# A two-layer attention and retention trunk on one core: the last projection's pairs prepared earlier, its weights' sums in three supertiles, the final squares in SBUF

## The chip, the core and the metric

The kernel runs on one core of a Trainium2 chip. The core has TensorE (PE in the profile: matmuls, and PEld for the loading of their stationary operand), VectorE (DVE), ScalarE (ACT), GpSimd (POOL), and SyncE (SP), whose queue issues all of this kernel's DMAs. Every engine works through its own instructions in order; they meet at semaphores. The metric is device time in microseconds, the median of several executions; less is better.

## The reference, cut to what matters

```python
def hybrid_layer(x, norm_gain, w_in, w_out, rel_bias, cos, sin):
    hn = rms_norm(x, norm_gain)
    proj = hn @ w_in
    aq, ak, av, ag, rq, rk, rv, rg = jnp.split(proj, cuts, axis=-1)
    ya = chunked_rel_attention(aq, ak, av, rel_bias)          # 8 heads x 64
    yr = chunkwise_retention(rq, rk, rv, cos, sin)            # 4 heads x 128
    y = jnp.concatenate([ya * silu(ag), yr * silu(rg)], axis=-1)
    return x + y @ w_out

def reference(x, positions, norm_gain, w_in, w_out, rel_bias, final_gain):
    cos, sin = rotary_tables(positions, RET_HEAD_DIM)
    for layer in range(2):
        x = hybrid_layer(x, norm_gain[layer], w_in[layer], w_out[layer], rel_bias[layer], cos, sin)
    return rms_norm(x, final_gain)
```

2048 tokens, model width 1024, w_in 1024 x 4096 and w_out 1024 x 1024 for each layer.

## The kernel before

Every dense product is made of three f16 matmuls (upper half by upper half, upper by lower, lower by upper) that sum in f32 in PSUM. The tokens are cut into 16 tiles of 128 and four supertiles of 512 (`n` = 0 to 3). A layer runs over four groups of heads (`s` = 0 to 3), and in each over the supertiles: `dense_T` (12 rounds of 8 matmuls), then `dense_V` (12 rounds). `run` steps such a generator, and with each of its rounds one step of the attention of the supertile before (`attention`, 24 steps; 8 units of a token tile and a head), one step of what `later` has put off, and one step of a background generator from `push`, which prepares weights. So the instructions of PE, ACT, DVE and POOL stand in an order written out by hand, round by round. SP's order is the scheduler's, except that DMAs wrapped in `in_turn` keep their program order.

An attention unit puts its scores in PSUM (tile `S`, one buffer; line 838), DVE moves them out (849), ACT makes the exponentials (852, 854), POOL the lower halves (855), a DMA transposes them (857), PE multiplies by v (865 to 867), DVE divides and gates (877), and the result goes to `y_d` in DRAM (880; retention's at 958).

The last layer's projection, `x + y @ w_out`, is made of two-by-two blocks with seven products instead of eight (`PRODS`, line 1192). For it a *pair* is two token tiles; there are 8 pairs, and each of the seven products of a pair is 12 matmuls of 512 columns. `fast_out` runs pair after pair in `R` = 12 rounds of 7 matmuls each. Its seven left operands are blocks of y or sums of them (`A11`, `A22`, `S1`, `S2`, `S5`, `S6`, `S7`). The chain that makes a pair's operands:

- `pair_y`: two loads of y from `y_d` (1243); `pair_x`: two of x (1310).
- `sq`: ACT squares y and sums (1256); `scale`: five small operations on DVE (1260 to 1263); `mul`: ACT scales y (1268).
- `sum`: POOL makes the five sums (1286). `rows`: ACT makes the f16 upper half of a block (1296) in a tile of a ring of three (`tabc`, `tabs`, `swp`; `rowring`). `lower`: DVE, for `S1` POOL, makes the lower half (1300). `turn`: a DMA transposes both halves (1303) into one of two areas `u.T`, used by even and odd pairs; the eighth block of an area is `u.spare`.

The products are taken out of PSUM by DVE (`add_to`, 1431) and, for a second use of four of them, by ACT with an add on POOL (`by_copy`, 1438 and 1439). `final` then squares and sums the finished tile on ACT (212), with a result that nobody reads (`junk`) in a PSUM tile of tag `S`, takes the root on DVE and POOL (217, 219), scales on DVE (1018) and stores (1019).

In `fast_out` the dictionary `plan` (1392) says in which round of pair p a step of the chain of pair p + 1 stands: `sq` in rounds 0 and 1, the `turn`s in rounds 5 to 11, the loads of x in 8, and in 9 and 10 the loads of y for pair p + 2. The chain of pair 0 is made by `pair_first`, in the background of supertile 3 of the last group. With `slow` = 2 the attention of that supertile takes one step in every second round of `fast_out`: 48 rounds, pairs 0 to 3.

The right operands are blocks of w_out and their sums. `fast_weights` makes three big tiles of them (`B11`/`D21`, `T6`/`B22`, `T1`/`T7`) in the background of supertile 2: for each of four column parts two loads of 512 KB, four operations on POOL (1213, 1215, 1216), three on ACT (1220), three on DVE (1222). `pair_first` makes `D12` in supertile 3, with a difference on POOL (1326).

Of the kernel before, what the change touches and what calls it, by code (L numbers as in the profile page):

```python
# [27 lines left out]
def hybrid_trunk(ctx: ExitStack, tc: tile.TileContext, x, pos, gain, gcol, w_in, w_out, rel, fgain,  # L28
# [794 lines left out]
    def attention(l, s, n, g, st, prev):  # L823
# [36 lines left out]
        def pv(u):  # L860
            t = 4 * n + u.a
            o = psR.tile([P, 512], F32, tag="small", name=f"o{u.nm}")
            for b, (q_, a_) in enumerate(u.kts):
                v_ = q_.v[:, a_, u.hx, :]
                pe.matmul(o[:, 0:65], u.p[:, b, :], v_[:, 0:65], start=(b == 0), stop=False)  # L865
                pe.matmul(o[:, 0:64], u.p[:, b, :], v_[:, 65:129], start=False, stop=False)  # L866
                pe.matmul(o[:, 0:65], u.p[:, u.nb + b, :], v_[:, 0:65], start=False, stop=(b == u.nb - 1))  # L867

            def out_():
                rl = b2.tile([P, 1], F32, tag="rl", name=f"rl{u.nm}")  # L870
                dve.reciprocal(rl, o[:, 64:65])  # L871
                dve.tensor_tensor(rl, rl, g.ka, op=ALU.mult)
                if u.hx == 0:
                    ya[u.a] = b2.tile([P, P], F32, tag="ya", name=f"ya{u.nm}")
                y = ya[u.a]
                vs = slice(u.hx * 64, u.hx * 64 + 64)
                dve.scalar_tensor_tensor(out=y[:, vs], in0=o[:, 0:64], scalar=rl[:, 0:1], in1=st.g[u.a][:, vs],
                                         op0=ALU.mult, op1=ALU.mult)
                if u.hx == 1:
                    later(1, lambda: in_turn(sp.dma_start(y_d[t][:, s * P:(s + 1) * P], y)))  # L880

            later(1, out_)
# [3 lines left out]
        for i, (a, hx) in enumerate(units):  # L886
            flow(1)
            u = qk(a, hx)
            for r in range(3 * i, 3 * i + 3):
# [4 lines left out]
                yield  # L894


    def products(out_, pairs):
# [11 lines left out]
    def retention(l, s, n, g, st):  # L909
        for a in range(4):  # L910
# [43 lines left out]
            def fin(t=t, a=a, r2=r2, ss=ss, nm=nm):  # L954
                y = b1.tile([P, P], F32, tag="yr", name=f"yr{nm}")
                dve.scalar_tensor_tensor(out=y, in0=r2[:, 0:P], scalar=ss[:, 0:1], in1=st.g[a][:, P:256],
                                         op0=ALU.mult, op1=ALU.mult)
                later(1, lambda: in_turn(sp.dma_start(y_d[t][:, 512 + s * P:512 + (s + 1) * P], y)))

# [234 lines left out]

    def fast_weights(l, fw, go):

        big = [hT[l, 0], hT[l, 1], (b3.tile([P, KT, 512], F16, tag="wh", name=f"whF{l}"),
                                    b3.tile([P, KT, 512], F16, tag="wl", name=f"wlF{l}"))]
        h = KT // 2
        for (hi, lo), names in zip(big, (("B11", "D21"), ("T6", "B22"), ("T1", "T7"))):  # L1200
            for i, nm in enumerate(names):
                fw.w[nm] = (hi[:, i * h:(i + 1) * h, :], lo[:, i * h:(i + 1) * h, :])
        for j in range(4):
            js = slice(j * P, (j + 1) * P)
            st = []
            for c in range(2):
                st += load_sec(w_out[l, :, c * 512 + j * P:c * 512 + (j + 1) * P], f"F{l}_{j}{c}")
            st = [st_[0] for st_ in st]
            yield
            yield  # L1210
            tm = w4.tile([P, KT, P], F32, tag="w4", name=f"tmF{l}_{j}")
            for k in range(2):
                pool.tensor_tensor(tm[:, k * h:(k + 1) * h], st[0][:, k * h:(k + 1) * h], st[1][:, h:KT], op=ALU.add)
            yield
            pool.tensor_tensor(st[0][:, h:KT], st[0][:, h:KT], st[0][:, 0:h], op=ALU.subtract)
            pool.tensor_tensor(st[1][:, 0:h], st[1][:, 0:h], st[0][:, 0:h], op=ALU.add)
            srcs = (st[0], st[1], tm)
            for i in range(4):
                if i < 3:
                    act.activation(big[i][0][:, :, js], srcs[i], AF.Copy, scale=go.os[:, 0:1])  # L1220
                if i > 0:
                    dve.scalar_tensor_tensor(out=big[i - 1][1][:, :, js], in0=srcs[i - 1], scalar=go.os[:, 0:1],
                                             in1=big[i - 1][0][:, :, js], op0=ALU.mult, op1=ALU.subtract)
                if i < 3:
                    yield

# [7 lines left out]
    def pair_y(l, u, k):  # L1234
        t = u.t + k
        if k == 0:
            u.y = []
# [20 lines left out]
    def pair_scale(u, k, go):  # L1258
        m = u.m[k]
        dve.tensor_scalar(m, m, 2.0 ** -100, None, op0=ALU.max)  # L1260
        sy, iy = norm_scale(m, f"{u.nm}_{k}", None, 13)
        sc = b2.tile([P, 1], F32, tag="osc", name=f"osc{u.nm}_{k}", bufs=4)
        dve.tensor_tensor(sc, iy, go.oi, op=ALU.mult)
        u.s.append(sy)
        u.sc.append(sc)

# [44 lines left out]

    def pair_first(l, u, fw, go, areas):

# [10 lines left out]
        def diff(j):  # L1324
            a = st[j]
            pool.tensor_tensor(a[:, 0:h], a[:, 0:h], a[:, h:KT], op=ALU.subtract)

# [53 lines left out]

    def fast_out(l, fw, go, u, areas):

        NP = NT // 2
        R = 12
        events = {}
        nxt = pair(l, 1)
        for k in range(2):
            pair_y(l, nxt, k)
        pair_x(l, u)  # L1390
        mm = [(i, kt, w) for i in range(7) for kt in range(KT // 2) for w in range(3)]
        plan = {0: (("sq", 0),), 1: (("sq", 1), ("scale", 0)), 2: (("scale", 1), ("mul", 0)), 3: (("mul", 1), ("rows", "A11")),
# [29 lines left out]
        for p in range(NP):  # L1422
            if nxt is not None:
                pair_area(nxt, areas)
            after = pair(l, p + 2) if p + 2 < NP else None
            x1, x2 = u.x
# [14 lines left out]
            for r in range(R):  # L1441
                for fn in events.pop((p, r), ()):
                    fn()
                if ring["att_done"] and r % 3 == 1:
                    flow()
                assert r != 9 or p < 4 or ring["att_done"]
                for what, k in plan[r]:
                    if what == "y":
                        if after is not None:
                            pair_y(l, after, k)  # L1450
                    elif nxt is not None:
                        steps[what](nxt, k)

# [4 lines left out]
                for m in range(7 * r, 7 * r + 7):  # L1458
# [31 lines left out]
                    elif i == 5:  # L1490
                        add_to(x1, 0, ps, s1)
                        final(u.t, x1, at)
                    else:
                        add_to(x2, 1, ps, s2)
                        final(u.t + 1, x2, at)
                yield
            u, nxt = nxt, after
        for key in sorted(events):
# [249 lines left out]
    for l in range(DEPTH):  # L1748
# [4 lines left out]
        for s in range(NSW):  # L1753
            g = grp(l, s)
            for n in range(NS):
# [37 lines left out]
                if last:  # L1793
# [3 lines left out]
                    else:  # L1797
                        u0 = pair(l, 0)
                        push(pair_first(l, u0, fw, go, areas), 24)
                if not first:  # L1800
# [14 lines left out]
        if l + 1 == DEPTH:  # L1815
            ring["fg"] = cp.tile([P, D], F32, tag="gb", name="fg")
            sp.dma_start(ring["fg"], fgain.to_broadcast([P, D]))
            run(fast_out(l, fw, go, u0, areas), att, 96, 2)
            continue
# [80 lines left out]
```

## Time and profile before

| | us |
|---|---|
| median of 3 runs | 2153.07 |
| lowest and highest run | 2149.65, 2157.38 |
| the profiled execution's own time | 2152.09 |
| its span, first to last instruction | 2150.3 |

| engine | busy us | share of the span |
|---|---|---|
| PE | 1998.6 | 93% |
| DVE | 1297.6 | 60% |
| ACT | 1192.0 | 55% |
| POOL | 827.3 | 38% |

The last supertiles of the last group lie at about 1715 to 1777 us (n = 1), 1777 to 1838 us (n = 2) and 1838 to 1901 us (n = 3); `fast_out`'s first product starts at 1901.0 us and its last matmul at 2136.7 us. These bounds are read from the first and last instructions of lines 1213 (1777.4 us), 1326 (1852.7 us) and 1469 (1901.0 us). The views used below: the busy times by stretch (columns: stretch in us, its length, busy us of PE, PEld, DVE, ACT and POOL with instruction counts, granted PE clock, share of the DMA engines, GB/s); the waits (who waited for whom: total us, times, longest); the timeline (start us, duration us, engine, line, operation, and in brackets the idle time before with what ended it); the groups of instructions by line (busy us, mean ns, idle before); and the answers for one line or tile (duration ns min/median/max).

### The profile page before, as it was taken

The numbers are of one execution on the slowest core, as the hardware profiler recorded it, in microseconds if no ns is written. First come the engines' busy times: TensorE is split into PE (matmuls) and PEld (weight loads), VectorE is DVE, ScalarE is ACT, GpSimd is POOL, SyncE is SP. The second block draws the span as 40 slices with busy tenths as digits, with TensorE's granted clock in tenths as the row PEclk, the third lists the DMA queues.
The fourth block names the chain that finished last, engine by engine and source line by source line (L and its number), as shares of the span: only waits on it lengthen the run. The fifth ranks groups of instructions, "written<-read, shape, count | busy, mean of one in ns | idle before, by whom it ended". The sixth has DMA issues, their size and how long they took to land. (4 is left out here: it accounts for less than half of the span.)

```text
span 2150.3 us, 39602 instructions
## 1 busy us (share of the span) xinstructions
PE 1998.6 (93%) x13930; PEld 1046.4 (49%) x13930; DVE 1297.6 (60%) x3877; ACT 1192.0 (55%) x2622; POOL 827.3 (38%) x800
## 2 busy tenths in 40 slices
PE   6898999999999999989999999999999998876676
PEld 4444455555555555444445555555555554433332
DVE  7776656565556556766535565556556646656565
ACT  7556665465656545555445465556665645555444
POOL 1333333334433343310024433443334436554554
PEclk9999999999999999999999999999999999998888
DMA  8787765555676556998655475547485635756675
GB/s 230 166 165 161 159 136 123 115 142 127 140 162 154 129 118 124 201 254 236 185 142 121 101 156 118 115 105 155 117 184 115 150 83 134 167 136 172 154 192 146
DMA packets 675208, 322.05 MB, mean 150 GB/s; under 512 B 484640, under 2 KB 631584, under 8 KB 675008
## 3 DMA queue, kind: packets, MB, share of 16 engines
q1 hardware_dynamic: 675008, 319.51, 64.7%
q8 instruction: 109, 1.79, 0.4%
q14 instruction: 91, 0.75, 0.1%
HBM read 125.36 MB, written 41.98 MB: 78 GB/s over the span
## 5 line engine op out<-in xcount | busy, mean ns | idle before, releaser
L855 POOL TENSOR_TENSOR pq<-sc,pq 128x640 f16<-128x640 f32 (+4 forms) x256 | 321.2, 1255 | 859.5 <-ACT pq L854 469.2
L852 ACT ACTIVATE sc<-sc,mq,cT 128x640 f32<-128x640 f32 (+4 forms) x256 | 218.4, 853 | 597.9 <-DVE rl L871 273.3
L797 PE MATMUL dV<-whV,hTh 128*128 128x512 f16 x1024 | 353.3, 381 | 12.1 <-DVE gt L815 9.4
L778 PE MATMUL dT<-hTh,whT 128*128 128x512 f16 x1008 | 348.3, 381 | 6.0 <-DVE gt L815 2.8
L797 PE MATMUL dV<-whV,hTl 128*128 128x512 f16 x1024 | 353.1, 380 | 0.0
L797 PE MATMUL dV<-wlV,hTh 128*128 128x512 f16 x1024 | 352.9, 380 | 0.0
L778 PE MATMUL dT<-hTl,whT 128*128 128x512 f16 x1008 | 346.6, 379 | 0.0
L778 PE MATMUL dT<-hTh,wlT 128*128 128x512 f16 x1008 | 346.6, 379 | 0.0
L797 PEld LDWEIGHTS <-hTh 128*128 128x128 f16 x2048 | 196.7, 98 | 226.3 <-DVE gt L815 12.3
L778 PEld LDWEIGHTS <-whT 128*128 128x128 f16 x2016 | 192.5, 98 | 211.8 <-issue 3.3
L849 DVE CUSTOM_DVE_ANT_0 sc<-S,bias 128x640 f32<-128x640 f32 (+4 forms) x256 | 188.3, 735 | 84.8 <-PE S L846 83.1
L854 ACT ACTIVATE pq<-sc 128x640 f16<-128x640 f32 (+4 forms) x256 | 171.5, 670 | 8.1
L845 PE MATMUL S<-k,q 128*128 128x128 f16 (+3 forms) x592 | 143.9, 269 | 32.0 <-ACT fj L212 30.5
L797 PEld LDWEIGHTS <-hTl 128*128 128x128 f16 x1024 | 99.3, 98 | 113.5 <-issue 4.6
L778 PEld LDWEIGHTS <-wlT 128*128 128x128 f16 x1008 | 97.2, 98 | 114.2 <-issue 6.8
L865 PE MATMUL o<-v,pT 128*128 128x65 f16 x1120 | 130.5, 194 | 18.0 <-DVE ssf L217 9.9
L865 PEld LDWEIGHTS <-pT 128*128 128x128 f16 x1120 | 106.0, 97 | 55.8 <-DMA pT<-pq 12.9
L952 POOL TENSOR_TENSOR rss<-rss,mhalf 128x1 f32<-128x1 f32 x128 | 74.8, 585 | 147.1 <-DVE rss L951 139.0
L846 PE MATMUL S<-k,q 128*128 128x128 f16 (+3 forms) x592 | 131.3, 270 | 0.0
L866 PE MATMUL o<-v,pT 128*128 128x64 f16 x1120 | 130.7, 195 | 0.0
L867 PE MATMUL o<-v,pT 128*128 128x65 f16 x1120 | 129.9, 193 | 0.0
L811 DVE SCALAR_TENSOR_TENSOR v<-dV,v 128x128 f16<-128x128 f32 x128 | 36.5, 285 | 140.6 <-ACT rv L807 129.8
(489 smaller groups left out, 4016.9 us busy)
## 6 DMA issues: line engine op xcount, KB each, us to landing
q<-qq SPq DMA_DIRECT2D x128, 128.0 KB, 2.4
stT<-in_w_in_dram SPq DMA_DIRECT2D x27, 512.0 KB, 4.8
stV<-in_w_in_dram SPq DMA_DIRECT2D x26, 512.0 KB, 4.6
k<-kk SPq DMA_DIRECT2D x128, 64.0 KB, 2.0
swp<-rot SPq DMA_DIRECT2D x64, 128.0 KB, 3.0
tabc<-tab SPq DMA_DIRECT2D x32, 256.0 KB, 3.0
tabs<-tab SPq DMA_DIRECT2D x32, 256.0 KB, 3.1
swp<-raw SPq DMA_DIRECT2D x64, 128.0 KB, 2.3
```

Of the source, the lines that this page charges most:

```text
L778: pe.matmul(ps, w_[:, j, kt, :], h_[:, kt, :], start=(m == 0), stop=(m == 23))
L797: pe.matmul(ps, h_[:, kt, a * P:(a + 1) * P], w_[:, kt, :], start=(m == 0), stop=(m == 23))
L845: pe.matmul(o, st.q[:, hx, 0, cs], k_, start=True, stop=False)
L846: pe.matmul(o, st.q[:, hx, 1, cs], k_, start=False, stop=True)
L849: dve.tensor_tensor_reduce(out=v, in0=S[:, 0:w], in1=g.bias[hx][:, 640 - w:640], scale=1.0, scalar=-3.0e38, op0=ALU.add, op1=ALU.max, accu ...
L852: act.activation(v, v, AF.Exp, bias=m[:, 0:1], scale=g.c[:, 0:1])
L854: act.activation(pq[:, 0:w], v, AF.Copy)
L855: pool.tensor_tensor(pq[:, w:2 * w], v, pq[:, 0:w], op=ALU.subtract)
L865: pe.matmul(o[:, 0:65], u.p[:, b, :], v_[:, 0:65], start=(b == 0), stop=False)
L866: pe.matmul(o[:, 0:64], u.p[:, b, :], v_[:, 65:129], start=False, stop=False)
L867: pe.matmul(o[:, 0:65], u.p[:, u.nb + b, :], v_[:, 0:65], start=False, stop=(b == u.nb - 1))
L952: pool.tensor_tensor(ss, ss, mhalf, op=ALU.pow)
```

## The change

1. Chains. `plan` becomes a list of steps with a round for each, laid out for all pairs ahead of the loop (`todo`). Pair 1 keeps its rounds (its loads of y move into `pair_first`, rounds 17 and 18); the chains of pairs 2 to 5 stand six rounds earlier than before, those of 6 and 7 four rounds earlier; every `turn` stands one round later than its chain otherwise moved (that of `S6` two), pair 1's too. The loads of x stay in round 8.
2. The ring for row tiles gets a fourth tile (`qq`). The squares' junk of `pair_sq` and of `final` goes to `u.spare` (f16, SBUF). The two scales of a pair share one tile, so four pairs' scales can live at once.
3. The last attention takes two steps in five rounds (60 rounds, pairs 0 to 4) in place of one in two. `y_parts` and the `assert` only count what was issued while the program is built.
4. Weights. `fast_weights` runs in two parts. Part 0, in supertile 1: `T1`/`T7` and `B11`/`D21`, from two loads of 512 KB for each column part; the two sums are on DVE, one difference on POOL. Part 1, in supertile 2: `T6`/`B22`, from a load of 512 KB and one of 256 KB (again of w_out), one sum on POOL. `D12`'s difference in `pair_first` moves from POOL to DVE.

```diff
-    def final(t, xt, at):
+    def final(t, xt, at, junk=None):
         def sq():
-            return squares(xt, f"f{t}", psS.tile([P, D], F32, tag="S", name=f"fj{t}"))
+            return squares(xt, f"f{t}", junk)
...
-    def fast_weights(l, fw, go):
+    def fast_weights(l, fw, go, part):
...
         for j in range(4):
...
-            for k in range(2):
-                pool.tensor_tensor(tm[:, k * h:(k + 1) * h], st[0][:, k * h:(k + 1) * h], st[1][:, h:KT], op=ALU.add)
-            yield
-            pool.tensor_tensor(st[0][:, h:KT], st[0][:, h:KT], st[0][:, 0:h], op=ALU.subtract)
-            pool.tensor_tensor(st[1][:, 0:h], st[1][:, 0:h], st[0][:, 0:h], op=ALU.add)
...
+            s0, s1 = load(j)
+            yield
+            yield
+            if part == 0:
+                tm = w4.tile([P, KT, P], F32, tag="w4", name=f"tmF{l}_{j}")
+                for k in range(2):
+                    dve.tensor_tensor(tm[:, k * h:(k + 1) * h], s0[:, k * h:(k + 1) * h], s1[:, h:KT], op=ALU.add)
+                yield
+                act.activation(big[0][0][:, :, j * P:(j + 1) * P], tm, AF.Copy, scale=go.os[:, 0:1])
+                pool.tensor_tensor(s0[:, h:KT], s0[:, h:KT], s0[:, 0:h], op=ALU.subtract)
+                yield
+                low(0, j, tm)
+                up(1, j, s0)
+                yield
+                low(1, j, s0)
+                yield
+            else:
+                yield
+                pool.tensor_tensor(s1[:, 0:h], s1[:, 0:h], s0, op=ALU.add)
+                yield
+                up(0, j, s1)
+                yield
+                low(0, j, s1)
+                yield
...
-            tag = ("tabc", "tabs", "swp")[rowring[0] % 3]
+            tag = ("tabc", "tabs", "swp", "qq")[rowring[0] % 4]
...
         def diff(j):
             a = st[j]
-            pool.tensor_tensor(a[:, 0:h], a[:, 0:h], a[:, h:KT], op=ALU.subtract)
+            dve.tensor_tensor(a[:, 0:h], a[:, 0:h], a[:, h:KT], op=ALU.subtract)
...
+        add(17, lambda: pair_y(l, us[1], 0))
+        add(18, lambda: pair_y(l, us[1], 1))
...
+        plan = (("y", 0, -3), ("y", 1, -2), ("area", 0, 0), ("sq", 0, 0), ("sq", 1, 1), ("scale", 0, 1), ("scale", 1, 2),
+                ("mul", 0, 2), ("mul", 1, 3), ("rows", "A11", 3), ("lower", "A11", 4), ("rows", "A22", 4), ("sum", "S2", 4),
+                ("turn", "A11", 5), ("lower", "A22", 5), ("rows", "S2", 5), ("sum", "S1", 5), ("sum", "S6", 5),
+                ("turn", "A22", 6), ("lower", "S2", 6), ("sum", "S7", 6), ("sum", "S5", 6), ("turn", "S2", 7),
+                ("rows", "S5", 7), ("lower", "S5", 8), ("rows", "S1", 8), ("turn", "S5", 9), ("lower", "S1", 9),
+                ("rows", "S7", 9), ("turn", "S1", 10), ("lower", "S7", 10), ("rows", "S6", 10), ("turn", "S7", 11),
+                ("lower", "S6", 11), ("turn", "S6", 12))
+        todo = {}
+        vs = us[0:2] + [pair(l, q) for q in range(2, NP)]
+        for q in range(1, NP):
+            for what, k, r in plan[2 if q == 1 else 0:]:
+                r_ = max(r + (what == "turn") + 12 * (q - 1) - (0 if q == 1 else 6 if q < 6 else 4), 0)
+                todo.setdefault(r_, []).append((vs[q], what, k))
+            todo.setdefault(12 * q - 4, []).append((vs[q], "x", 0))
...
-                 "sq": lambda v, k: pair_sq(v, k, v.T[BLOCKS[k]].rearrange("p k c -> p (k c)"))}
+                 "sq": lambda v, k: pair_sq(v, k, v.spare.rearrange("p k c -> p (k c)"))}
...
-                        final(u.t, x1, at)
+                        final(u.t, x1, at, u.spare.rearrange("p k c -> p (k c)"))
...
-    def run(gen, att, thirds, slow=1):
+    def run(gen, att, thirds, pace=5):
...
-            if att[0] is not None and i % slow == 0 and next(att[0], att) is att:
+            if att[0] is not None and i * pace % 5 < pace and next(att[0], att) is att:
...
-                if (l + 1, s, n) == (DEPTH, NSW - 1, 2):
-                    push(fast_weights(l, fw, go), 24)
+                if (l + 1, s) == (DEPTH, NSW - 1) and n in (1, 2):
+                    push(fast_weights(l, fw, go, n - 1), 24 if n == 1 else 20)
```

The call `run(fast_out(...), att, 96, 2)` keeps its last argument, which is now the pace.

More of the change, by code (lines that the diff above doesn't have):

```diff
@@ L879, in out_ @@
                 if u.hx == 1:
-                    later(1, lambda: in_turn(sp.dma_start(y_d[t][:, s * P:(s + 1) * P], y)))
+                    later(1, lambda: y_out(l, t, s * P, y))
             later(1, out_)
@@ new lines, in low, with load @@
+        def low(i, j, src):
+            hi, lo = (t_[:, :, j * P:(j + 1) * P] for t_ in big[i])
+            dve.scalar_tensor_tensor(out=lo, in0=src, scalar=go.os[:, 0:1], in1=hi, op0=ALU.mult, op1=ALU.subtract)
+        def load(j):
+            if part == 0:
+                return [load_sec(w_out[l, :, c * 512 + j * P:c * 512 + (j + 1) * P], f"F{l}_{part}{j}{c}")[0][0] for c in range(2)]
+            st = w4.tile([P, KT, P], F32, tag="w4", name=f"stE{l}_{j}")
+            sp.dma_start(st, w_out[l, :, 512 + j * P:512 + (j + 1) * P].rearrange("(k p) c -> p k c", p=P))
+            s0 = w4.tile([P, KT, P], F32, tag="w4", name=f"stF{l}_{j}")[:, 0:h]
+            sp.dma_start(s0, w_out[l, 0:h * P, j * P:(j + 1) * P].rearrange("(k p) c -> p k c", p=P))
+            return [s0, st]
@@ L1217, in fast_weights @@
[L1217 to L1225, printed above, removed]
+            if part == 0:
+                tm = w4.tile([P, KT, P], F32, tag="w4", name=f"tmF{l}_{j}")
[10 more added lines that the diff above has]
+                yield
+            else:
+                yield
[5 more added lines that the diff above has]
+                yield
@@ L1261, in pair_scale @@
         sy, iy = norm_scale(m, f"{u.nm}_{k}", None, 13)
-        sc = b2.tile([P, 1], F32, tag="osc", name=f"osc{u.nm}_{k}", bufs=4)
-        dve.tensor_tensor(sc, iy, go.oi, op=ALU.mult)
+        if k == 0:
+            sc = b2.tile([P, 2], F32, tag="osc", name=f"osc{u.nm}", bufs=4)
+            u.sc = [sc[:, i:i + 1] for i in range(2)]
+        dve.tensor_tensor(u.sc[k], iy, go.oi, op=ALU.mult)
         u.s.append(sy)
-        u.sc.append(sc)
     def pair_mul(u, k):
@@ L1422, in fast_out @@
         for p in range(NP):
-            if nxt is not None:
-                pair_area(nxt, areas)
-            after = pair(l, p + 2) if p + 2 < NP else None
+            u = vs[p]
             x1, x2 = u.x
@@ L1445, in fast_out @@
                     flow()
[L1446 to L1452, printed above, removed]
+                for v, what, k in todo.pop(p * R + r, ()):
+                    steps[what](v, k)
                 def at(k, fn, p=p, r=r):
```

43 lines of the change are left out of this document (21 added, 22 removed), and 7 rows, old and new, of the table plan.

## The prediction

> **What bounds the kernel now.** I read the stretches first, to see where PE idles; then the waits, to see on what; then the timeline around one such wait.
>
> ```profile
> span 2150.3 us, 39602 instructions
> ```
>
> ```profile
> core 0: us, PE busy (x) PEld busy (x) DVE busy (x) ACT busy (x) POOL busy (x), PEclk, DMA share, GB/s
> 1720.00:1778.00 58.00, 58.00 (x397) 29.98 (x395) 28.04 (x103) 26.22 (x71) 19.90 (x23) 1.00 0.35 79
> 1778.00:1838.00 60.00, 50.36 (x377) 26.23 (x374) 37.61 (x82) 30.77 (x57) 41.30 (x33) 1.00 0.62 138
> 1838.00:1901.00 63.00, 50.75 (x363) 26.21 (x361) 39.90 (x105) 35.14 (x75) 31.87 (x28) 0.95 0.67 162
> 1901.00:1937.00 36.00, 25.36 (x159) 12.22 (x157) 20.40 (x51) 18.16 (x34) 18.89 (x14) 0.95 0.67 151
> 1937.00:2062.00 125.00, 85.38 (x491) 41.54 (x491) 81.22 (x169) 62.45 (x110) 67.79 (x54) 0.84 0.65 166
> 2062.00:2137.00 75.00, 62.27 (x278) 27.80 (x276) 45.56 (x72) 34.05 (x57) 44.28 (x36) 0.91 0.70 179
> 1940.00:1960.00 20.00, 19.86 (x115) 9.65 (x114) 17.45 (x38) 13.09 (x24) 13.37 (x11) 0.95 0.64 156
> 1980.00:2000.00 20.00, 18.21 (x121) 9.17 (x119) 16.27 (x31) 11.22 (x19) 16.70 (x14) 1.00 0.46 112
> ```
>
> In supertile 1 (first row) PE is busy all the time: nothing is to be won there, only lost. Supertile 2 leaves PE idle for 60.0 - 50.4 = 9.6 us, supertile 3 for 12.3. In the projection pair 0 (1901 to 1937) leaves 10.6 us, pairs 1 to 4 (to 2062) 39.6 us of 125, pairs 5 to 7 12.7 us of 75. The projection is where the time is; its waits:
>
> ```profile
> PE S L845 <- ACT fj L212: 30.5, 3, 13.0
> PEld L865 <- DMA yTl<-rwz_4S: 10.3, 1, 10.3
> PE zz L1469 <- DMA yTh<-rwz_7A: 5.7, 1, 5.7
> PE zz L1469 <- DMA yTh<-rwz_6A: 5.3, 1, 5.3
> ACT rwz_3S L1296 <- DMA yTh<-rwz_3S: 10.2, 1, 10.2
> ```
>
> Three times PE stood before an attention unit's scores, 30.5 us in all, because the tile `S` was still the junk of a final square. The square itself is short; it came late. Around the longest such place but one, on ACT, PE and SP:
>
> ```profile
> 2009.09 0.63 ACT L1296 ACTIVATE rwz_3S<-yyz 128x512 f16<-128x512 f32 x1 [10.23 <-DMA yTh<-rwz_3S]
> 2009.63 1.01 ACT L212 ACTIVATE fj<-hTh 128x1024 f32<-128x1024 f32 x1
> ```
>
> ```profile
> 2010.82 0.27 PE L845 MATMUL S<-k,q 128*128 128x128 f16 x1 [12.61 <-ACT fj L212]
> ```
>
> ```profile
> 1992.26 1.23 SPq L1303 DMA_TRANSPOSE yTh<-rwz_3S  x1
> 2000.23 1.33 SPq L857 DMA_TRANSPOSE pT<-pq  x1
> 2001.65 1.02 SPq L1310 DMA_DIRECT2D hTl<-x_d  x2
> 2003.20 1.32 SPq L1303 DMA_TRANSPOSE yTh<-rwz_3S  x1
> ```
>
> ACT waited 10.23 us to write `S6`'s row tile, the ring's slot of `S5`, three tiles back. `S5`'s transpose was issued at 2003.20 only, behind an attention transpose and the loads of x, and landed at about 2009.1. The final square stood behind that `rows` on ACT, the scores behind the square. So one late transpose, through a ring of three and a shared PSUM tile, stops PE for 13 us; the 10.3 us wait before line 865 is the same ring stall of pair 4. Pairs 6 and 7, with no attention left, wait 5.3 and 5.7 us for their first operand itself. After a stall PE also runs slowly for a while:
>
> ```profile
> 1977.88 1.06 PE L1469 MATMUL zz<-hTh,yTh 128*128 128x512 f16 x2
> 1978.74 0.63 PE L1469 MATMUL zz<-hTl,yTh 128*128 128x512 f16 x1
> ...
> 1980.09 0.59 PE L1469 MATMUL zz<-hTh,yTh 128*128 128x512 f16 x2
> 1980.53 0.38 PE L1469 MATMUL zz<-hTl,yTh 128*128 128x512 f16 x1
> ```
>
> Two starts take 0.86 us there, 0.44 us later (0.216 us each). All products of the projection (8 x 84 of 512 columns) at 0.216 us would be 145 us; they occupied PE for 160.6 us:
>
> ```profile
> 1901.00:2137.00 236.00, 160.58 (x684) 43.92 (x60) 21.78 (x32) 0.88 0.67 168
> ```
>
> (the stretch's row for `zz` alone: PE, DVE, ACT). Some 15 us are slow clock; I put them down to the six stalls (three before line 845, one before 865, two before 1469), 2.5 us each.
>
> **Part by part: the squares, the ring and the earlier chains.** With junk in SBUF no scores wait for a square; with four slots `S6` takes `S2`'s, whose transpose was issued 11 us before `S5`'s (1992.26 against 2003.20); and with chains six rounds ahead (a round is 7 matmuls, 1.5 us) a late transpose meets a product that isn't due for five to ten rounds. All five PE waits above go. No work goes with them: the same squares, sums, halves and transposes remain, so the next limit is how densely the engines can be filled. Pairs 1 to 4 hold 81.2 us of DVE work, 0.65 x 125 = 81 us of DMA, 67.8 of POOL, and on PE 85.4, of which 10 are slow clock (four stalls). Three queues near 81 us cannot interleave perfectly. Between its stalls the kernel shows what it reaches: in 1940 to 1960 and 1980 to 2000, PE is at 99 and 91% and DVE at 87 and 81%, mean 84%. I take 81.2 / 0.84 = 96 us for the stretch: -29. Bounds: 81 (-44) if the queues pack fully, and 125 - 10 if only one stall in four leaves for good. The slower attention pace moves two of its eight units to later rounds; that is inside these bounds.
>
> Pairs 5 to 7: 62.3 us of PE, of which 5 slow clock (two stalls), DMA 0.70 x 75 = 52 us, DVE and POOL 45. Both waits (11 us) and the clock behind them go, and PE is the bound at about 57; I take 62: -13 (bounds -18 and -5). Pair 0 gets the first half of pair 2's chain beside pair 1's: its engines stand at 50 to 57% of 36 us, and I take 0 (bounds -5, half of its PE idle, and +6, a third of ACT's 18.2 us, should the half chain lie bare).
>
> What holds these lengths up is the price of two engines side by side:
>
> ```profile
> L1300 DVE TENSOR_TENSOR rwz_3A<-yyz,rwz_3A 128x512 f16<-128x512 f32 x2 | 3.4, 1752 | 0.0
> L1300 DVE TENSOR_TENSOR rwz_2S<-hTl,rwz_2S 128x512 f16<-128x512 f32 x2 | 1.4, 684 | 8.0 <-ACT rwz_2S L1296 8.0
> L1018 DVE SCALAR_TENSOR_TENSOR hTl<-hTl,rsf,fg 128x1024 f32<-128x1024 f32 x6 | 7.7, 1277 | 0.0
> L1286 POOL TENSOR_TENSOR S2z<-hTl 128x512 f32<-128x512 f32 x3 | 5.1, 1706 | 0.0
> L1286 POOL TENSOR_TENSOR yyz<-yyz 128x512 f32<-128x512 f32 x4 | 5.0, 1262 | 0.3
> ```
>
> A DVE half beside a POOL sum takes 1752 ns, alone 684; the sum 1706 and 1262. Denser work means more such meetings, which is why I stay off the lower bound. The Trainium skill (SBUF — State Buffer, "SBUF: two separate sides") says it more sharply: a DVE operation with two SBUF inputs and a GpSimd operation take the shared port pair in turn, each for its whole length. By that rule an estimate for pairs 1 to 4 adds POOL's 67.8 us, less 12 sums x 0.44 us of waiting, to 24 halves x 0.68 and 8 final scalings x 1.28 on DVE, 62.5 + 26.6 = 89 us, so that the stretch could not go under that and 81 would be out of reach. The rows agree with the rule in kind: 684 + 1262 = 1946 ns one after the other, 1752 side by side.
>
> **The weights.**
>
> ```profile
> L1213 POOL TENSOR_TENSOR tmF<-stF,stF x8: 1265/1267/1274, 1777.4 to 1832.5; 128x512 f32<-128x512 f32 x8
>   DMA stF<-in_w_out_dram: 3.8, 2
> ...
> L1215 POOL TENSOR_TENSOR stF<-stF x4: 1263/1267/1269, 1782.5 to 1836.0; 128x512 f32<-128x512 f32 x4
> ...
>   POOL stF L1215: 12.9, 4
> L1222 DVE SCALAR_TENSOR_TENSOR hTl<-stF,o_s,hTh x8: 1277/1284/2325, 1784.9 to 1841.3; 128x1024 f16<-128x1024 f32 x8
> L1326 POOL TENSOR_TENSOR stG<-stG x4: 1262/1266/1708, 1852.7 to 1876.3; 128x512 f32<-128x512 f32 x4
> 1824.17 0.39 PE L797 MATMUL dV<-whV,hTh 128*128 128x512 f16 x1 [3.23 <-DVE gt L815]
> ```
>
> (the fifth row is what line 1220 on ACT waited for). In supertile 2 POOL loses twelve of sixteen operations (15.2 us of 41.3) and DVE eight of twelve halves (10.3 of 37.6). The chain load, POOL sums, ACT, DVE half, then DVE's gate and PE behind it (3.23 us in the last row) shortens; I take -7 of the 9.6 us idle (bounds -9.6, -2). Supertile 3: POOL loses 4 x 1.27 us, DVE gains 4 x 0.7: -4 of 12.3 (bounds -8, +4), since its other waits are the retention's own. Supertile 1 gains on DVE 8 x 0.68 + 8 x 1.28 = 16 us on 28.0 of 58, on POOL 5, on ACT 9, and eight loads (4 MB, at 79 GB/s moved now). That lies beside PE's 58 us. Uncovered is the wait for a load, which now stands in DVE's queue instead of POOL's (3.8 us in two waits): behind it wait the score moves and the gates, and PE. I take +2 (bounds 0, +8). The 3 MB that are loaded more than before find DMA shares of 0.35 and 0.62. The two loads of y for pair 1 move past nothing that runs late: 0.
>
> **Sum.** -29 - 13 + 0 - 7 - 4 + 2 = -51 us. The profiled execution's own time is 2152.1 (span 2150.3, 1.8 around it), 1 us below the median of the runs. 2152.1 - 51 + 1 = 2102 us.
>
> **Rivals.**
> 1. *The engines don't pack: a new wait takes the place.* ACT's `rows S5` now stands in the same round distance behind POOL's five sums (1.26 to 1.71 us each, 8 us for two or three rounds), and `by_copy` behind it on ACT; or the transposes, 7 a pair with the attention's, queue on SP. For it: DMA is at 0.65 even with the stalls. Against it: six rounds of slack. If it keeps half of the gain of pairs 1 to 7 (21 us): 2102 + 21 = 2123.
> 2. *Full packing.* Pairs 1 to 4 at 83, 5 to 7 at 57, pair 0 and supertile 3 at their better bounds: 2102 - 13 - 5 - 5 - 4 = 2075. Against it: the meetings of DVE and POOL.
> 3. *Slower: DVE's waits for weights.* Twelve operations moved to DVE wait for or behind loads (eight sums in supertile 1, four differences in 3), in front of everything that empties PSUM. It decides when each costs PE over 53 / 12 = 4.4 us (53 is what the other terms win): at 5.5 us each, 66 - 53 = 13 us over the median, 2166. For it: POOL did wait 1.9 us a time, and a slot of three may free late. Against it: two or three rounds of cover.
> 4. *It doesn't do what it says:* the ring still stalls because the transposes stay as late as now (SP's order is the scheduler's), so the squares leave PE free but operands come as late. Only the weights (-9) and part of the stalls (some 13) remain: 2131; or, with nothing but the weights, no change within the measurement.
>
> **How the numbers follow.** Forecast 0.55 (2088 to 2114), rival 1 0.18, rival 2 0.12, rival 4 0.08 (of it 0.03 no change), rival 3 0.07. The range holds the forecast, rival 1 and most of rival 2, some 0.8: 2075 to 2129. 0.3% (6.5 us) is about what a measurement can tell from no change. Faster by more: 0.55 + 0.18 + 0.12 + 0.05 = 0.90; same 0.03; slower 0.07.
>
> **What would show it.** Right: no wait of line 845 for line 212; ACT's `rows` no longer waiting for a turn's DMA by 10 us; PE clock 1.00 through the projection; pairs 1 to 4 in 92 to 100 us with DVE over 80% busy; supertile 2 with under 4 us of PE idle. Wrong: a PE wait over 4 us at the start of a pair, DVE waiting for `stF` in supertile 1, PE under 97% there, or pair 0 over 42 us.

## The result and the profile after

The changed kernel takes 2125.70 us (median of 4 runs, 2124.48 to 2127.26), the kernel before, beside it on the same chip, 2152.32 us. The ratio is 0.9874 with a 95% interval of 0.9854 to 0.9894: 26.6 us faster, where 51 were forecast.

First the stretches of the changed kernel that answer to those of before (us, length, busy us of PE, PEld, DVE, ACT and POOL, granted PE clock, share of the DMA engines, GB/s): supertiles 1, 2 and 3, pair 0, pairs 1 to 4, the rest. The last row is that of the tile `zz` alone (PE, DVE, ACT).

```profile
span 2122.7 us, 39586 instructions
...
core 0: us, PE busy (x) PEld busy (x) DVE busy (x) ACT busy (x) POOL busy (x), PEclk, DMA share, GB/s
1715.00:1781.00 66.00, 59.69 (x388) 29.62 (x385) 41.49 (x115) 31.66 (x72) 27.71 (x25) 1.00 0.58 130
1781.00:1841.00 60.00, 52.72 (x387) 27.36 (x388) 33.70 (x92) 28.02 (x63) 24.85 (x22) 0.97 0.57 132
1841.00:1902.00 61.00, 51.63 (x375) 26.50 (x374) 39.12 (x109) 33.48 (x73) 28.19 (x25) 0.98 0.71 171
1902.00:1935.00 33.00, 24.69 (x124) 10.99 (x123) 22.44 (x58) 23.16 (x42) 17.92 (x14) 0.88 0.69 173
1935.00:2036.00 101.00, 84.29 (x482) 40.95 (x482) 78.64 (x147) 55.95 (x101) 71.55 (x55) 0.92 0.83 195
2036.00:2109.00 73.00, 61.46 (x303) 27.99 (x302) 47.90 (x86) 34.21 (x58) 43.83 (x35) 0.93 0.76 191
...
1902.00:2109.00 207.00, 158.09 (x668) 43.55 (x60) 21.71 (x32) 0.92 0.78 190
```

Supertile 1, where PE had no idle time, now has 6.3 us of it (66.0 - 59.7); supertile 2 has 7.3 (9.6 before) and supertile 3 9.4 (12.3 before). Together that is 23.0 us against 21.9: the weights won nothing. In the projection the clock is 0.88 to 0.93, not 1.00, and `zz` occupies PE for 158.1 us (160.6 before).

The exact starts of the pairs can be read from PE's timeline: the first four products of a pair read their left operands from the tiles `yTh`, the last three from `yTl`, so that a pair begins where the operand goes back from `yTl` to `yTh`. The table holds the lengths in us for the two kernels and for three of the runs below (one profiled execution each, differences of starts rounded to 0.1 us; the programs of columns 1, 3 and 4 are the same up to the projection and yet start it 3 us apart, so single profiles tell nothing finer than that).

| | before | after | before, ring and squares | the same, and turns later | after, two parts undone |
|---|---|---|---|---|---|
| projection starts at | 1901.0 | 1901.3 | 1901.2 | 1897.9 | 1903.0 |
| pair 0 | 31.0 | 35.4 | 32.5 | 32.5 | 33.8 |
| pairs 1 to 4 | 132.8 | 103.5 | 126.0 | 112.2 | 101.7 |
| pairs 5 to 7, to the last matmul of 512 columns | 68.6 | 67.7 | 69.8 | 62.5 | 63.4 |
| from there to the span's end | 16.9 | 14.8 | 15.6 | 16.8 | 16.3 |

Between the spans of before and after (27.6 us) lie +0.3 ahead of the projection, +4.4 in pair 0, -29.3 in pairs 1 to 4, -0.9 in pairs 5 to 7 and -2.1 behind them.

The waits of the changed kernel from 1895 us on, of PE and of ACT (who waited for whom: us in all, times, longest):

```profile
PE zz L1500 <- ACT cpz L1474: 9.9, 4, 5.7
PE zz L1500 <- DVE hTh L1467: 5.7, 3, 3.0
PE r L905 <- ACT cpz L1474: 5.6, 2, 2.9
PE o L865 <- DVE ssf L217: 5.2, 1, 5.2
...
ACT rwz_7S L1326 <- POOL yyz L1316: 7.6, 1, 7.6
ACT rwz_6S L1326 <- POOL hTh L1316: 7.4, 1, 7.4
ACT yTl L1285 <- DMA yyz<-y_d: 7.3, 3, 5.4
```

The three large waits of before (30.5 us for the squares, 10.3 before line 865, 11.0 for the first operands of pairs 6 and 7) are gone but for 5.2 us at line 865. What is left is many waits of 2 to 6 us, mostly for what takes the products out of PSUM (line 1474 is `by_copy` here, 1467 `add_to`, 1326 `rows`, 1316 `sum`, 1285 the squares of y, 1500 the products).

### The profile page after: what moved, and what is told of

Same layout as the page of the kernel before. It is cut to its first block, busy times and chain, and to the rows that moved or that the text cites. A ratio compares the mean times of both kernels' runs of the same rounds, so it can differ in the third digit from the quotient of the medians.

```text
span 2122.7 us, 39586 instructions
## 1 busy us (share of the span) xinstructions
PE 1999.4 (94%) x13930; PEld 1044.1 (49%) x13930; DVE 1302.7 (61%) x3889; ACT 1190.8 (56%) x2622; POOL 815.9 (38%) x788
```

## The experiments

### Parts taken back from the changed kernel

**The squares back in PSUM.** In `final`:

```diff
-            return squares(xt, f"f{t}", junk)
+            return squares(xt, f"f{t}", psS.tile([P, D], F32, tag="S", name=f"fj{t}"))
```

> The changed kernel with one thing undone: the final squares' junk is again a PSUM tile of tag S, shared with the scores. If the ring of four and the earlier chains alone keep the squares in time (theory), PE waits under 3 us in all before line 845, and the time is 2126 to 2130 us. If the shared tile was the cause of the stalls (rival), PE waits 15 to 30 us there again and the time is 2140 to 2155 us.

2127.54 us (2124.84 to 2129.42): at most 2 us are lost, and PE has no wait before line 845 that the profile lists. Once the squares come in time, it doesn't matter where their result goes.

**No lead.** The chains of pairs 2 to 7 in the same rounds as before; the turns stay a round later than before:

```diff
-                r_ = max(r + (what == "turn") + 12 * (q - 1) - (0 if q == 1 else 6 if q < 6 else 4), 0)
+                r_ = max(r + (what == "turn") + 12 * (q - 1), 0)
```

> The changed kernel with the chains of pairs 2 to 7 in the rounds of before (no six or four rounds of lead; turns one round later as in the change). If the lead is what shortens pairs 1 to 4 (theory), PE waits for first operands at the starts of pairs and the time is 2135 to 2145 us. If the ring and the junk in SBUF do it alone (rival), the time stays at 2123 to 2129 us.

2130.04 us (2128.06 to 2133.24), between the two forecasts. The rounds of lead, which give the change its name, are worth some 4 us; 20.7 of the gain (2150.73 for the kernel before in these runs) are there without them.

**The weights as before**, all in supertile 2 on POOL, `D12`'s difference on POOL too:

```diff
-                if (l + 1, s) == (DEPTH, NSW - 1) and n in (1, 2):
-                    push(fast_weights(l, fw, go, n - 1), 24 if n == 1 else 20)
+                if (l + 1, s, n) == (DEPTH, NSW - 1, 2):
+                    push(fast_weights(l, fw, go), 24)
```

> The changed kernel with the weights as before: all three big tiles made in supertile 2 with sums on POOL, D12's difference on POOL. If the new placement gives back in supertile 1 what it wins in 2 and 3 (theory), the time is 2122 to 2129 us. If it pays the 9 us of the prediction (rival), it is 2133 to 2136 us.

2123.84 us (2123.38 to 2124.47), no slower than with them. **The sums of supertile 1 on POOL**, the rest as changed:

```diff
-                    dve.tensor_tensor(tm[:, k * h:(k + 1) * h], s0[:, k * h:(k + 1) * h], s1[:, h:KT], op=ALU.add)
+                    pool.tensor_tensor(tm[:, k * h:(k + 1) * h], s0[:, k * h:(k + 1) * h], s1[:, h:KT], op=ALU.add)
```

> The changed kernel with the two sums of part 0 (T1/T7, eight operations in supertile 1) back on POOL, all else as changed. If DVE's two sums of 0.68 us in front of the retention's dT cost PE its three waits of 1.6 to 1.9 us in supertile 1 (theory), these waits go and the time falls by 4 to 6 us, to 2120 to 2122 us. If the waits come from the halves or from late loads (rival), the time stays within 2 us of 2125.7.

2122.13 us (2121.51 to 2127.33), 3.6 less, which by itself the intervals don't settle; a second pair of runs below shows 2.8 in the same direction. Why DVE is the wrong place for these sums stands in the changed kernel's timeline of DVE and PE in supertile 1 (start us, duration us, engine, line, operation, and the idle time before with what ended it):

```profile
1742.36 1.29 DVE L1236 TENSOR_TENSOR tmF<-stF,stF 128x512 f32<-128x512 f32 x2 [4.57 <-DMA stF<-in_w_out_dram]
1743.57 0.34 DVE L962 SCALAR_TENSOR_TENSOR yr<-r,rss,gt 128x128 f32<-128x128 f32 x1
1743.83 0.28 DVE L913 SCALAR_TENSOR_TENSOR dT<-dT,r 128x128 f16<-128x128 f16 x1
...
1744.16 0.23 PE L905 MATMUL r<-rv,dT 128*128 128x128 f16 x1 [1.63 <-DVE dT L913]
```

DVE waits 4.57 us for the load, then makes both sums, and only then the small retention operation for which PE stands by (5.1 us in three such waits in this supertile). The step of the weights repeats every six rounds and so does the retention's, so each pair of sums meets the same spot: PE waits at 1744.16, 1758.15 and 1774.09 us, for three of the four pairs of sums. Only the first of them has a late load ahead of it. With the sums on POOL these waits shrink from 5.1 us to 1.0.

**The ring of three** in the changed kernel:

```diff
-            tag = ("tabc", "tabs", "swp", "qq")[rowring[0] % 4]
+            tag = ("tabc", "tabs", "swp")[rowring[0] % 3]
```

> The changed kernel with the row tiles' ring of three again. If the chains' lead and the squares in SBUF already take the sting out of a late transpose (theory), it stays at 2124 to 2130 us. If the ring of three was the root of the stalls (rival), ACT waits 10 us in four pairs again and the time is 2138 to 2150 us.

2126.75 us (2126.27 to 2128.28): 1 us, within the spread of the runs. ACT's longest wait for a turn is 4.3 us, not 10.

**The old pace** of the last attention, one step in two rounds:

```diff
-            run(fast_out(l, fw, go, us, areas), att, 96, 2)
+            run(fast_out(l, fw, go, us, areas), att, 96, 2.5)
```

> The changed kernel with the last attention's old pace, one step in two rounds (48 rounds, pairs 0 to 3). If the pace is worth nothing by itself (theory), 2123 to 2129 us. If the attention in pair 4 and the late loads of y for pair 6 behind it cost pair 5 its wait of 5.2 us (rival), pair 5 falls from 27 to some 20 us and the time to 2117 to 2121 us.

2120.79 us (2116.52 to 2122.53): 5 us faster than the change with its slower pace. A part of what the pace costs is to be seen in the final scalings on DVE (line 1024). Two groups for the changed kernel, then the same two for the run with the old pace (ns: shortest/median/longest, first and last start):

```profile
L1024 DVE SCALAR_TENSOR_TENSOR hTh<-hTh,rsf,fg x8: 1275/1786/2283, 1945.2 to 2102.5; 128x1024 f32<-128x1024 f32 x8
L1024 DVE SCALAR_TENSOR_TENSOR hTl<-hTl,rsf,fg x7: 1285/2281/2368, 1974.8 to 2117.8; 128x1024 f32<-128x1024 f32 x7
```

```profile
L1024 DVE SCALAR_TENSOR_TENSOR hTh<-hTh,rsf,fg x8: 1274/1324/2282, 1949.1 to 2100.3; 128x1024 f32<-128x1024 f32 x8
L1024 DVE SCALAR_TENSOR_TENSOR hTl<-hTl,rsf,fg x7: 1275/1327/2280, 1977.5 to 2115.6; 128x1024 f32<-128x1024 f32 x7
```

With the slower pace 11 of these 15 scalings take over 1.6 us, with the old pace 5; in all they take 28.8 us against 24.5. Mostly it is the engine that starts second that is held up: at 1945.20 us of the changed kernel a scaling began 0.2 us after a POOL operation and took 2.16 us; at 1949.14 with the old pace one began 0.2 us ahead of a POOL operation and took 1.27. (Two that began only 0.01 to 0.02 us ahead took 2.36 and 2.37.) The Trainium skill (SBUF — State Buffer, "SBUF: two separate sides") has a DVE operation with two SBUF inputs and a GpSimd operation exclude each other; these durations agree, 2.37 being a little under 1.27 and a POOL sum of 1.26 one after the other. That the 5 us come from there isn't shown. In the profiles most of them lie in pairs 5 to 7, which take 63.9 us instead of 67.7; pair 5 itself takes 23.6 instead of 27.0, not the 20 that the rival named.

So nothing that was taken back by itself from the changed kernel cost more than some 4 us. The gain had to lie in something that was still in it each time, or in parts that stand in for each other.

### Parts added to the kernel before

**The fourth row tile alone:**

```diff
-            tag = ("tabc", "tabs", "swp")[rowring[0] % 3]
+            tag = ("tabc", "tabs", "swp", "qq")[rowring[0] % 4]
```

> The kernel before with one thing added: the fourth tile in the ring. If the ring is the root of the stalls (theory), ACT's waits of 10 us and PE's before line 845 go, and the time is 2128 to 2135 us. If the late transposes stall something else at once (rival), 2143 us or more.

2146.47 us (2144.97 to 2149.15), 6.4 faster, as the rival had it. From its waits:

```profile
ACT yTh L1256 <- DMA hTh<-y_d: 17.7, 3, 8.6
ACT yTh L1256 <- DMA yyz<-y_d: 16.9, 5, 7.1
...
PE S L845 <- ACT fj L212: 7.6, 2, 3.8
PEld L1469 <- DMA yTh<-rwz_7A: 6.5, 1, 6.5
PEld L1469 <- DMA yTh<-rwz_6A: 6.1, 1, 6.1
```

ACT waits for no ring tile any more, but 34.6 us for loads of y in these two rows, where the kernel before waited 3.2 (1.7 and 1.5). The ring had only stood in front of the next late thing.

**The squares in SBUF alone** (in `final`, with the pair's `spare` as junk):

```diff
-                        final(u.t, x1, at)
+                        final(u.t, x1, at, u.spare.rearrange("p k c -> p (k c)"))
```

> The kernel before with one thing added: the final squares' junk in SBUF. ACT still waits 10 us for the ring in four pairs. If PE only meets the next thing that ACT holds up, a PSUM tile that isn't copied out (theory), the time is 2140 to 2150 us. If the shared tile alone did the harm (rival), 2128 to 2134 us.

2150.12 us (2147.12 to 2154.67), 2.8 faster, at the upper end of the theory's range. Its waits:

```profile
PE zz L1469 <- DVE ya L877: 26.3, 3, 11.5
ACT rwz_1S L1296 <- DMA yTh<-rwz_1S: 10.3, 1, 10.3
```

The 30.5 us for the squares became 26.3 us for a PSUM tile that DVE had not emptied: PE stops at the same place for a different reason, since ACT still waits 10 us for the ring.

**Both edits together:**

> The kernel before with two parts of the change at once: the fourth row tile in the ring and the final squares' result in SBUF; chains, turns, pace and weights as before. Alone the ring gave 6.4 us and the squares 2.8. Theory (they are two links of one chain: with the ring alone the scores still stand behind late squares, with the squares alone the ring still holds ACT for 10 us): together they give clearly more than their sum, 2130 to 2138, and neither scores wait for a square nor does ACT wait 10 us for a turn. Rival (the loads of y and the turns are late by themselves, and whatever waits first is only a different engine): no more than the sum, 2142 to 2146, with ACT waiting for y loads as long as with the ring alone (33 us in 8 waits).

2147.21 us (2145.70 to 2149.90), 4.8 faster: no more than the ring gave alone. The time is 1 us above the rival's range, and its mechanism holds: ACT waits as long for loads of y as with the ring alone. Its waits, and SP's queue at the turn of pair 5's `S5` (the first `rwz_5S` here is `S2`, the second `S5`; line 1310 loads x, 1243 loads y, here for pair 6):

```profile
PE zz L1469 <- DVE ya L877: 22.3, 3, 9.5
ACT yTh L1256 <- DMA hTh<-y_d: 18.0, 3, 8.6
ACT yTh L1256 <- DMA yyz<-y_d: 17.1, 4, 7.3
```

```profile
2057.93 1.23 SPq L1303 DMA_TRANSPOSE yTh<-rwz_5S  x1
2059.25 1.02 SPq L1310 DMA_DIRECT2D hTl<-x_d  x2
2063.41 1.23 SPq L1303 DMA_TRANSPOSE yTh<-rwz_5S  x1
2064.69 0.57 SPq L1243 DMA_DIRECT2D hTh<-y_d  x1
```

SP issues nothing between 2060.3 and 2063.4 us: it stands before the turn of `S5`, which needs POOL's five sums, ACT's half and DVE's half. The load of y for pair 6 stands behind it and goes out at 2064.69, 5.0 us after pair 5 has begun. Pair 6's squares, with which its chain begins, wait for it. At the turns of pairs 1 to 4 the order is the same, with an attention transpose ahead of all, and there it is this transpose that SP stands before (6.5 us at the turn of pair 3, until 1998.36); behind it come the loads of x and the turn, and the load of y for pair 4 goes out at 2002.71.

How such a late load stops PE can be seen at that load, on SP, ACT, DVE and PE (`rwz_3S` is `S5`'s turn here, line 857 the attention's transpose):

```profile
1998.36 1.32 SPq L857 DMA_TRANSPOSE pT<-pq  x1
...
2001.33 1.33 SPq L1303 DMA_TRANSPOSE yTh<-rwz_3S  x1
2002.71 0.69 SPq L1243 DMA_DIRECT2D hTh<-y_d  x1
```

```profile
2008.21 1.06 ACT L1256 ACTIVATE yTh<-hTh 128x1024 f16<-128x1024 f32 x1 [7.37 <-DMA hTh<-y_d]
```

```profile
2009.39 0.15 DVE L1260 TENSOR_SCALAR ymz<-ymz 128x1 f32<-128x1 f32 x1 [6.92 <-ACT yTh L1256]
...
2011.53 0.28 DVE L877 SCALAR_TENSOR_TENSOR ya<-o,rl,gt 128x64 f32<-128x64 f32 x1
```

```profile
2011.96 0.58 PE L1469 MATMUL zz<-hTh,yTh 128*128 128x512 f16 x1 [9.51 <-DVE ya L877]
```

The squares of y wait for the load, DVE's scale (1260) waits for the squares' sum, behind it in DVE's order stands the attention's division that empties a PSUM tile (877), and PE waits 9.5 us for that tile.

**And the turns one round later**, on top of the two (`S6`'s two rounds, as in the change; chains, pace, weights and loads as before):

```diff
+                for v, k in turns.pop(p * R + r, ()):
+                    pair_turn(v, k)
                 for what, k in plan[r]:
...
-                    elif nxt is not None:
+                    elif nxt is not None and what != "turn":
                         steps[what](nxt, k)
+                    elif nxt is not None:
+                        turns.setdefault(p * R + r + 1 + (k == "S6"), []).append((nxt, k))
```

> The kernel before with the fourth row tile and the squares' result in SBUF, and, new, the turns of pairs 1 to 7 one round later (that of S6 two), as the change places them; chains, pace, weights and the loads of y where they were before. Without the turns' move this kernel took 2147.2 us, and the changed kernel without the six rounds of lead 2130.0. Theory (in SP's queue the turn of S5 stood just ahead of the first load of y for the pair after next, both in round 9, and waits there for POOL's five sums; one round later it lets the load past, so the next pair's squares start in time): 2130 to 2137, ACT's squares of y wait for loads of y under 15 us in all (35 in the run without the move), and pairs 6 and 7 wait under 5 us each for their first operand (6.6 and 6.6). Rival (the attention's pace or the earlier loads for pair 1 did it): 2143 to 2149, loads of y as late as without the move.

2124.78 us (2123.08 to 2128.42; ratio to the kernel before 0.9878, 0.9862 to 0.9895): 22.4 us from this edit by the medians, more than the theory had, and as fast as the whole change. (The profiles differ by 23.2, of which 3.3 lie ahead of the projection, where the two programs are alike.) Its waits and the same place in SP's queue:

```profile
ACT yTh L1256 <- DMA yyz<-y_d: 8.0, 3, 3.8
PE zz L1474 <- DVE ya L877: 7.0, 2, 5.9
...
PEld L1474 <- DMA yTh<-rwz_6A: 4.4, 1, 4.4
...
ACT yTh L1256 <- DMA hTh<-y_d: 3.7, 1, 3.7
```

```profile
2041.24 1.01 SPq L1310 DMA_DIRECT2D hTl<-x_d  x2
2042.30 0.42 SPq L1243 DMA_DIRECT2D hTh<-y_d  x1
2046.54 1.24 SPq L1303 DMA_TRANSPOSE yTh<-rwz_5S  x1
```

The load of y has changed places with the turn. It goes out 0.3 us before pair 5 begins (2042.6), and SP stands before the turn afterwards, with the second load of y behind it, for which ACT does not wait here. ACT's waits for loads of y fall from 35.1 to 11.7 us, DVE's waits for the squares (line 1260) from 37.6 to 17.0, PE's for line 877 from 22.3 to 7.0. It is the same in every pair: the squares began 13.0, 13.1, 13.2, 9.5 and 11.0 us after the starts of pairs 2 to 6, and now begin after 11.0, 10.7, 10.6, 7.6 and 8.8; and these pairs are 1.8 to 3.5 us shorter each.

The edit moved more in SP's queue than the turn, since the scheduler orders the transposes anew. Around pair 1's turn the first load of y went ahead of the attention transpose as well:

```profile
1920.62 0.43 SPq L1243 DMA_DIRECT2D hTh<-y_d  x1
1925.53 1.33 SPq L857 DMA_TRANSPOSE pT<-pq  x1
```

The squares of pair 2's chain now begin 2.5 us before pair 1 instead of 6.2 after its start, and pair 1 became 5.2 us shorter. Around the turns of pairs 2 to 4 the loads of x went ahead of that transpose, and SP still stands before it (5.6 us at pair 3's); there the load of y goes out 2.0 us after the transpose instead of 4.4. All turns were moved in this run, so the share of `S5`'s own turn, and of these other moves, isn't measured; nor was the move tried without the ring and the squares, or taken back from the changed kernel.

### Two combinations

**The old pace and the sums on POOL together**, both edits as above in the changed kernel:

> The kernel after with two of its parts taken back: the last attention takes one step in two rounds, and the two sums of the weights in supertile 1 are on POOL. Alone they gave 5 and 3.5 us. Theory (they lie in different stretches, the sums before 1901 us and the pace in the projection): they add up, 2115 to 2119. Rival (both free the same DVE queue ahead of the last attention): 2120 to 2122.

2117.95 us (2115.25 to 2120.52; ratio to the kernel before 0.9835, 0.9818 to 0.9851). The two add up: 7.8 us less than the whole change, and the fastest kernel of the study.

**ACT's row tiles in the order of POOL's sums**, on top of that:

```diff
-                ("rows", "S5", 7), ("lower", "S5", 8), ("rows", "S1", 8), ("turn", "S5", 9), ("lower", "S1", 9),
-                ("rows", "S7", 9), ("turn", "S1", 10), ("lower", "S7", 10), ("rows", "S6", 10), ("turn", "S7", 11),
-                ("lower", "S6", 11), ("turn", "S6", 12))
+                ("rows", "S1", 7), ("lower", "S1", 8), ("rows", "S6", 8), ("turn", "S1", 9), ("lower", "S6", 9),
+                ("rows", "S7", 9), ("turn", "S6", 10), ("lower", "S7", 10), ("rows", "S5", 10), ("turn", "S7", 11),
+                ("lower", "S5", 11), ("turn", "S5", 12))
```

> The kernel of the run before in this list (two parts taken back), and ACT's row tiles in the order in which POOL makes their sums: S1, S6, S7, S5 in rounds 7 to 10 instead of S5, S1, S7, S6, each lower half one round and each turn two rounds after. Theory (rows S5 behind all five sums holds ACT for 7 us in pairs 6 and 7, and by_copy behind it holds PE): 3 to 6 us less than the run before, and no wait of ACT's rows for POOL over 3 us. Rival (the wait falls on slack of the chain, PE's waits at 1500 come from the scalings and by_copy themselves): within 2 us of the run before, PE's wait for ACT's cpz as long.

2125.04 us (2123.48 to 2128.86): 7 us slower, which neither side expected. ACT's `rows` no longer wait 7.6 us for POOL, but `by_copy` waits for DVE 48.6 us in 18 times (25.7 and 22.9) instead of 29.7 in 14. PE's own wait for these copies is about as long (10.7 us for 12.0), as the rival had it. Some of the loss lies elsewhere: `S5`, the fourth operand that a pair needs, now comes last, and PE waits 1.7 and 2.4 us for it in pairs 6 and 7. Why DVE comes later was not found out.

## Why the prediction was right, and where it was not

**The direction and the stretch were right.** Faster was given 0.90, the time lies in the range, and pairs 1 to 4 became 29.3 us shorter against a forecast of 29. The large waits named were the right ones, and they went. That 29.3 and 29 agree is luck: the forecast took the 125 us from 1937 to 2062 for pairs 1 to 4, while by the pairs' starts they last 132.8 us (1932.0 to 2064.8), and it expected 96 us where 103.5 came. DVE fills 77% of these, not 84.

**The cause was named a step too late in the chain.** The prediction said that one late transpose, through the ring of three and the shared PSUM tile, stops PE, and gave the gain to the squares, the ring and the six rounds. Ring and squares together gave 4.8 us, the rounds 4. The transpose was late itself, and it made the loads behind it late; the part that mends this, "every turn one round later", was described in the change and costed nowhere. It gave 22.4 on top of the ring and the squares. The wait before line 865 was read wrongly for the same reason: put down to the ring, it stayed at 9.6 us of PE's time with ring and squares (9.9 before) and fell to 5.9 with the turns later. The row was at hand: the timeline of SP quoted there shows the queue's order down to the turn at 2003.20, and the loads of y stand next. Rival 4 came near: it let the operands stay late if the transposes did. With ring and squares alone that is what happened; its price, 2131, was too low, because it counted 13 us for the stalls, where ring and squares gave 4.8, and 9 for the weights, which gave nothing.

**Pairs 5 to 7: -13 forecast, -3.0 measured** (-0.9 to the last matmul, -2.1 behind it). The waits for the first operands went, but two of the same size came. The changed kernel's ACT and PE in pair 7's chain and after:

```profile
2086.61 0.63 ACT L1326 ACTIVATE rwz_7S<-yyz 128x512 f16<-128x512 f32 x1 [7.58 <-POOL yyz L1316]
2087.14 0.67 ACT L1474 ACTIVATE cpz<-zz,oscz 128x512 f32<-128x512 f32 x1
...
2091.15 0.58 PE L1500 MATMUL zz<-hTh,yTh 128*128 128x512 f16 x1 [5.67 <-ACT cpz L1474]
```

`rows` of `S5` waits for POOL's sums, the copies out of PSUM stand behind it on ACT, and PE waits 5.67 us for a free tile at 2091.15, the start of pair 7. This is rival 1's mechanism as it was told. That the late `rows` makes PE's wait isn't shown: with ACT's row tiles in the order of the sums that wait went, and PE waited about as long for the copies. The other is the wait of 5.2 us at line 865: the slower pace leaves attention in pair 5, which had none before (27.0 us instead of 23.9; 23.6 with the old pace in the changed kernel). The forecast left both out, and the time is nearer to rival 1's 2123 than to 2102.

**The weights: -9 forecast, about 0 measured.** Supertiles 2 and 3 gave 2.3 and 2.9 us of PE's idle time for 7 and 4. Supertile 1 lost 6.3 for 2: inside its bounds. The wait for a load that was named for it stands ahead of one of PE's three waits for the retention; the other two come from the sums' own length. With the old weights the time is the same.

**Pair 0: 0 forecast, +4.4 measured**, inside the bounds. ACT has 23.2 us of work in 33 where it had 18.2 in 36: the half chain does lie partly bare.

**The pace was not costed** ("inside these bounds"); it costs 5 us. **The clock** was to come back with the stalls, 15 us; `zz` lost 2.5 at most (the products are as many as before, but the profile after has 668 records of them for 684). The granted clock of the projection went from 0.88 to 0.92 only, with many short waits in place of six long ones.

**What speaks against the forecast's list:** no wait of line 845 for line 212 and no 10 us wait of `rows`, as said; but DVE at 78% in pairs 1 to 4 (78.6 of 101), not over 80, those pairs in 103.5 us, not under 100, and three of its four signs of error: a wait over 4 us at a pair's start, DVE waiting for `stF` in supertile 1, and PE at 90% there. Pair 0 stayed under 42.

## What to carry to other kernels

When a chain is late, follow the waits one link further than the engine that stops: what stood ahead of the late DMA in its issuing queue, and what stands behind it. A DMA that is put into an in-order queue before its data are ready holds every load behind it; moving the turns one round down, past the loads, was worth 22 us here, on top of two buffers that had been added for the symptom and gave 5 without it. Each part that was undone alone cost 4 us at most, and the turns' place was not among them; adding parts to the old kernel found it.

## What the runs showed of the hardware

An issuing queue is a place where time is lost that no engine's busy time shows: SP stood idle 3.1 us before one turn, with a load behind it that another order issued first. The Trainium skill (DMA: Bandwidth & Descriptors, "Issuing engines are not separate DMA queues") says that issuing from several engines saves only the sequencer's time for starting a DMA, usually small beside the transfer. The rows above show a second thing that a queue costs, the wait for a DMA that isn't ready; whether a second issuing engine would have saved it was not tried.

Two instruction streams with the same period can meet at the same place every time: sums of 1.29 us on DVE stood before the retention's step at all four of their turns, and PE waited at three. And the length of a DVE operation over two SBUF inputs depended for the most part on whether a POOL operation was running when it started: the final scalings took from 1.27 us to 2.37, and a different pace of a third stream, the attention, moved the number of those over 1.6 us from 5 of 15 to 11.
